# A hybrid attention, Fourier and long-convolution block: two opening blocks of one tile, the context's squares from its columns, and its norm factor ahead of the second filter's transform

## The chip, the core and the metric

The kernel runs on one core of a Trainium2 chip. A core has a matmul engine (TensorE, PE in the profile, with its weight loads as PEld), a vector engine (VectorE, DVE), an engine for activations and copies (ScalarE, ACT), a general engine (GpSimd, POOL) and a queue engine that issues most transfers (SyncE, SP). Each engine takes its instructions in a fixed order and waits where an operand is not there yet. Matmuls add up in PSUM, in eight banks of 128 x 512 fp32; everything else lies in SBUF, 128 partitions wide. The metric is the device time of one launch in microseconds; lower is better.

## The reference

One layer of a backbone over 256 latent tokens and 256 context tokens, 2048 channels wide, one sample, all in fp32. The change lies in the first step for both token sets, and in the filters of the long convolution:

```python
def rmsnorm(x, g):
    xf = x.astype(jnp.float32)
    y = xf * lax.rsqrt(jnp.mean(xf * xf, axis=-1, keepdims=True) + EPS)
    return (y * g.astype(jnp.float32)).astype(x.dtype)

def modulate(h, shift, scale):
    return h * (1 + scale) + shift

mod = (silu(c) @ ada_w + ada_b)            # 6 parts of 2048: sh1, sc1, g1, sh2, sc2, g2
mod_c = silu(c_ctx) @ ada_w + ada_b
h = modulate(rmsnorm(x, norm1_g), sh1, sc1)
hc = modulate(rmsnorm(ctx, norm1_g), csh1, csc1)
q, k, v, f, hy = split_projection(h @ w_in)
kc, vc = split(hc @ w_in[:, 1024:3072])
a = neighbourhood_attention(q, k, v, kc, vc, rpb)     # window keys and all context keys
y = merge_groups(a, fourier_mix(f), hyena_mix(hy, ...), mix_norm_g)
x = x + g1 * (y @ w_out)
x = x + g2 * conv_gated_mlp(modulate(rmsnorm(x, norm2_g), sh2, sc2), ...)
return rmsnorm(x, final_norm_g)
```

`hyena_mix` has two long convolutions. Each one's filter comes from a small sine network with a decay, and is used through its spectrum.

## The kernel before

Activations lie with channels on partitions: 16 tiles of 128 channels by 256 tokens. Every fp32 weight chunk is split in two by ScalarE (`w_hi`, a rounded copy, L173) and VectorE (`w_lo`, the rest, L174); an activation is split likewise (`hx_hi`, `hx_lo` of the latents, `hc_hi`, `hc_lo` of the context), and a product is three matmuls (`mm3`, L162).

The opening stage, which the change touches, makes keys and values for both token sets. It runs over blocks of channel tiles, `blocks=(2, 2, 4, 4, 4)`. For each block, the modulation (shift and scale of these channels) is first worked out from raw chunks of `ada_w`, in pieces (`prep_pieces`; products at L496 in four strips of 32 rows, `adasb` at L506, transposes at L170, the columns A1 and B1 at L515 and L516). Then `hprep` makes the activations of the block: `modulate` (L252, the tile `ht`), then `hi` on ScalarE (L256) and `lo` on VectorE (L257). Then four groups (`group`) multiply the block's tiles: two of keys, two of values. The first block's results are copied out of PSUM (L581), later ones added (L583). The pieces of the next block stand among the groups of the present one. A block of nk tiles takes 2 MB of modulation chunks for two tiles' width, and 1 MB of weights for each tile.

Ahead of the blocks stands a list of steps, `start` in `CFG`. `x0 x1` load the latents as pairs of tiles, `a00 a01 a10 a11` the first block's modulation chunks, `W` its first weights, `ct` the context a second time, by rows of tokens (2 MB into `kT`), `c0 c1` the context by channels. `q0` sums the latents' squares on PE through a matrix of ones; `q1` sums the context's by rows, with ScalarE's own accumulator (L461, `c_sq`). `n0` and `n1` make the norm factors; `n1` makes a factor for each token, and spreads it over partitions through a diagonal matrix `dg` (L226) and a matmul, to `rs_b` (L231). `f0` and `f1` make the two filters in time (`kz`, in the tile `v_t`, L436), and `s0` and `s1` their spectra (`fold`, four matmuls against `ftab`, a copy at L181 and four adds and subtractions at L184 to L188). `h0` and `h1` are `hprep` of the first block for the latents and the context, `e` a piece of its modulation, `w` its first weight split. A scheduler orders each engine's instructions from this list and their dependencies, so rows of one step stand between those of another.

Raw chunks of 512 KB go through eight buffers (`w_raw`) and three set aside for some modulation chunks (`a_raw`); a buffer is free when its chunk has been multiplied or split. Split weights have two buffers. SP issues loads in one order, and a load whose buffer is not free holds up all behind it. Sums in PSUM use five banks (`acc_ps`) and three (`mi_ps`).

After this stage come the other projections, the Fourier and long-convolution groups, attention, the output projection and the MLP, all on the same pattern. Another part of the modulation is made on VectorE (`ada_cols`, L351) beside the matmuls, and reads `s_row`, a row of activated conditions spread over partitions (`silu_row`, issued before the second block).

## Time and profile before

| | us |
|---|---|
| median of three runs | 1295.93 |
| lowest, highest | 1295.56, 1326.62 |
| the profiled execution | 1301.22 |
| its span | 1299.4 |

The profiled execution is one of its own, 5.3 us over the median of the runs. Its span runs from the first instruction to the last; 1.8 us lie around it.

| stage, us from the span's start | PE busy, us | granted clock | GB/s |
|---|---|---|---|
| 0 to 20 | 14.89 | 1.00 | 320 |
| 20 to 30 | 8.95 | 0.83 | 419 |
| 30 to 40 | 10.00 | 1.00 | 411 |
| 40 to 50 | 5.30 | 0.95 | 343 |
| 50 to 60 | 10.00 | 0.71 | 213 |
| 60 to 80 | 20.00 | 1.00 | 303 |
| 80 to 100 | 20.00 | 1.00 | 396 |

The columns come from windows of the profile. Busy time of PE counts the whole span of a matmul, with what its pipeline overlaps, so a full window does not mean that matmuls follow as closely as they can; the granted clock is the share of full speed at which PE may run. An fp32 matmul that is not split shows as two records. Rows of a timeline are: start, length, engine, line, operation, tile written and tiles read, count, and in brackets the idle time of the engine ahead of it with what ended it.

### The profile page before, as it was taken

What the parts mean: (1) busy time and instruction counts of PE and PEld (TensorE: products, weight loads), DVE (VectorE), ACT (ScalarE), POOL (GpSimd) and SP (SyncE); (2) the same over time, 40 slices, a digit from 0 to 9 for tenths busy, and PEclk for the clock granted to TensorE, in tenths of its full rate; (3) what the DMA queues carried; (4) which work ended last, traced back from release to release, by engine and by line L of the source; (5) the groups of instructions that cost most, each with busy time, mean ns of one, the idle gap of its engine ahead of it and who ended that gap; (6) DMA issues with size and microseconds to landing.
All of it is one profiled execution on the core that took longest, in us unless ns stands there. A gap on an engine that the chain in (4) does not pass through costs nothing.

```text
span 1299.4 us, 24490 instructions
## 1 busy us (share of the span) xinstructions
PE 1271.8 (98%) x10290; PEld 1197.3 (92%) x10290; DVE 886.5 (68%) x1301; ACT 558.5 (43%) x736; POOL 0.9 (0%) x7
## 2 busy tenths in 40 slices
PE   8899999999989999999999999999999999999997
PEld 5578788899989888999999999999999999999997
DVE  4447668958999897987676767744446555655663
ACT  4443212135333665455444444433334444454543
POOL 0000000000000000000000000000000000000000
PEclk9899999999999999999999999999999999999999
DMA  9887888988669875846877777855555656665541
GB/s 357 331 338 262 313 333 300 339 277 306 213 235 342 305 233 172 275 150 220 274 251 265 254 262 256 293 195 194 193 194 192 194 193 195 193 195 192 195 162 66
DMA packets 94015, 315.28 MB, mean 243 GB/s; under 512 B 16080, under 2 KB 16336, under 8 KB 93264
## 3 DMA queue, kind: packets, MB, share of 16 engines
q1 hardware_dynamic: 93328, 312.65, 69.5%
q8 instruction: 80, 1.31, 0.4%
q10 hardware_dynamic: 576, 1.07, 0.2%
q14 instruction: 31, 0.25, 0.1%
HBM read 311.58 MB, written 2.10 MB: 241 GB/s over the span
## 4 chain that ended last, share of the span: by engine, by line
PE 90%; DVE 5%; DMA 2%; ACT 1%; issue 1%; DVEq 0%; SPq 0%; ACTq 0%
PE acc_ps L162 83%; PE mi_ps L162 4%; PE mi_ps L496 2%; DVE w_lo L174 1%; DMA raw<-in_ada_col_t 1%; PE mi_ps L170 1%; DMA raw<-in_ada_t 1%; DVE raw L351 1%; DMA x_in<-in_xT 0%; ACT w_hi L173 0%; DMA hpack<-in_hpack 0%; DVE Y L768 0%; PE acc_ps L496 0%; DVE X L775 0%; DVE X L184 0%
## 5 line engine op out<-in xcount | busy, mean ns | idle before, releaser
L173 ACT CAST w_hi<-raw 128x1024 fp32r<-128x1024 f32 x376 | 381.1, 1051 | 524.2 <-PE acc_ps L162 457.6
L174 DVE TENSOR_TENSOR w_lo<-raw,w_hi 128x1024 fp32r<-128x1024 f32 x376 | 448.3, 1222 | 221.2 <-ACT w_hi L173 220.4
L162 PE MATMUL acc_ps<-h_hi,w_hi 128*128 128x256 f32 x1408 | 388.3, 276 | 0.5 <-ACT h_hi L256 0.5
L162 PE MATMUL acc_ps<-h_lo,w_hi 128*128 128x256 f32 x1408 | 388.6, 276 | 0.0
L162 PE MATMUL acc_ps<-h_hi,w_lo 128*128 128x256 f32 x1408 | 388.5, 276 | 0.0
L162 PEld LDWEIGHTS acc_ps<-h_hi,w_hi 128*128 128x128 f32 x1408 | 264.1, 188 | 0.7 <-ACT h_hi L256 0.7
L162 PEld LDWEIGHTS acc_ps<-h_lo,w_hi 128*128 128x128 f32 x1408 | 264.3, 188 | 0.0
L162 PEld LDWEIGHTS acc_ps<-h_hi,w_lo 128*128 128x128 f32 x1408 | 264.3, 188 | 0.0
L162 PE MATMUL acc_ps<-yh,w_lo 128*128 128x256 f32 x704 | 194.3, 276 | 0.0
L162 PE MATMUL acc_ps<-yh,w_hi 128*128 128x256 f32 x704 | 194.3, 276 | 0.0
L162 PE MATMUL acc_ps<-yl,w_hi 128*128 128x256 f32 x704 | 194.3, 276 | 0.0
L351 DVE SCALAR_TENSOR_TENSOR raw<-raw,s_row 128x1024 f32<-128x1024 f32 x128 | 154.8, 1223 | 39.1 <-DMA raw<-in_ada_col_t 39.0
L162 PE MATMUL acc_ps<-hx_hi,w_hi 128*128 128x256 f32 x512 | 145.6, 285 | 0.0
L162 PE MATMUL acc_ps<-hx_hi,w_lo 128*128 128x256 f32 x512 | 142.6, 281 | 1.0 <-DVE w_lo L174 1.0
L162 PE MATMUL acc_ps<-hx_lo,w_hi 128*128 128x256 f32 x512 | 143.2, 280 | 0.0
L162 PEld LDWEIGHTS acc_ps<-yh,w_hi 128*128 128x128 f32 x704 | 132.2, 188 | 0.0
L162 PEld LDWEIGHTS acc_ps<-yl,w_hi 128*128 128x128 f32 x704 | 132.2, 188 | 0.0
L162 PEld LDWEIGHTS acc_ps<-yh,w_lo 128*128 128x128 f32 x704 | 132.2, 188 | 0.0
L162 PEld LDWEIGHTS acc_ps<-hx_hi,w_hi 128*128 128x128 f32 x512 | 96.3, 188 | 8.1 <-issue 4.2
L162 PEld LDWEIGHTS acc_ps<-hx_lo,w_hi 128*128 128x128 f32 x512 | 96.5, 188 | 2.8 <-issue 2.4
L162 PEld LDWEIGHTS acc_ps<-hx_hi,w_lo 128*128 128x128 f32 x512 | 96.0, 189 | 2.1 <-DVE w_lo L174 1.4
L694 ACT ACTIVATE ga<-acc_ps,pack 128x256 f32<-128x256 f32 x44 | 23.8, 559 | 38.0 <-PE acc_ps L162 31.6
(237 smaller groups left out, 1532.0 us busy)
## 6 DMA issues: line engine op xcount, KB each, us to landing
raw<-in_ffn_t SPq DMA_DIRECT2D x264, 512.0 KB, 4.4
raw<-in_ada_col_t SPq DMA_DIRECT2D x128, 512.0 KB, 5.0
raw<-in_ada_t SPq DMA_DIRECT2D x64, 512.0 KB, 7.0
raw<-in_w_in_t SPq DMA_DIRECT2D x48, 512.0 KB, 5.5
raw<-in_w_kv_t SPq DMA_DIRECT2D x32, 512.0 KB, 5.9
raw<-in_w_out_t SPq DMA_DIRECT2D x32, 512.0 KB, 4.7
x_in<-in_xT SPq DMA_DIRECT2D x8, 256.0 KB, 5.4
kT<-in_c_tok SPq DMA_DIRECT2D x1, 2048.0 KB, 14.8
```

Of the source, the lines that this page charges most:

```text
L162: return nc.tensor.matmul(ps, lhsT, rhs, start=start, stop=stop, skip_group_check=True)
L170: nc.tensor.transpose(ps, src, ident[:n, :n])
L173: nc.scalar.copy(hi, src)
L174: TT(lo, src, hi.bitcast(F32), op=ALU.subtract)
L351: STT(r, r, 1.0, s_row[:, h * NA : (h + 1) * NA], op0=ALU.mult, op1=ALU.mult, accum_out=sums_[:, f, h : h + 1])
L496: return nc.tensor.matmul(ps[32 * j : 32 * j + 32, :w], s_t[:, kt, :], raws[i // nh][:, kt % nh, :], start=fresh, stop=q == last_q and i i ...
L694: nc.scalar.activation(dst, ps, AF.Identity, bias=b, scale=w1_)
```

## The change

The blocks become `(1, 1, 2, 4, 4, 4)`. A block of one tile takes one pair of modulation chunks for shift and one for scale, over 128 columns, and one weight chunk of 2048 columns, whose two halves are now columns and not tiles. The first two channel tiles of `x`, `ctx` and the low parts become tiles of their own, so that they can be used alone.

The load of the context by rows is gone. `q1` now squares the context's channel tiles on ScalarE and adds the squares on VectorE into one pair of tiles; `rms_bcast` then sums over channels with four matmuls against ones. In the list of steps `s1` moves from before `n1` to the end, behind `h1`; `ct`, `a01`, `a11` and two of the four `e` go.

```diff
-    p1=(0, 0, 2, 6, 9),
-    blocks=(2, 2, 4, 4, 4),
+    p1=(0, 0, 0, 2, 6, 9),
+    blocks=(1, 1, 2, 4, 4, 4),
...
-    start='hp pk x0 x1 h3 dc ft a00 a01 a10 a11 W wm si n1s wp n2s q0 ct c0 c1 e e n0 f0 e e h0 w s0 f1 s1 q1 n1 h1',
+    start='hp pk x0 x1 h3 dc ft a00 a10 W wm si n1s wp n2s q0 c0 c1 e n0 f0 e h0 w s0 f1 q1 n1 h1 s1',
...
         def add(self):
-            self.tiles.append(self.pool.tile([P, 2, L], self.dt, tag=self.pool.name, name=self.name, bufs=KT // 2))
+            if len(self.tiles) < 2:
+                t = self.pool.tile([P, 1, L], self.dt, tag=self.pool.name + "_1", name=self.name, bufs=2)
+            else:
+                t = self.pool.tile([P, 2, L], self.dt, tag=self.pool.name, name=self.name, bufs=KT // 2 - 1)
+            self.tiles.append(t)
...
-        def row_squares():
-            sums = p1.tile([P, 2], F32, name="c_sq")
-            for t in range(2):
-                nc.scalar.activation(c_tok[:, t], c_tok[:, t], AF.Square, accum_out=sums[:, t : t + 1])
-            return sums
+        def summed_squares():
+            for q in range(KT // 2):
+                sq = kT[:, q, :]
+                if q:
+                    nc.scalar.activation(sq.rearrange("p (k n) -> p k n", n=L), xs[1].tiles[q + 1][:], AF.Square)
+                    TT(kT[:, 0, :], kT[:, 0, :], sq, op=ALU.add)
+                else:
+                    for i in range(2):
+                        nc.scalar.activation(sq[:, i * L : (i + 1) * L], xs[1].tiles[i][:, 0], AF.Square)
+            return [kT[:, 0, i * L : (i + 1) * L] for i in range(2)]
...
-            rbs[v] = rms_bcast(p1, None, D, f"rs{v}", ps) if v else rms_rows(p1, ps[:, :L], D, f"rs{v}")
+            rbs[v] = rms_bcast(p1, ps, D, f"rs{v}") if v else rms_rows(p1, ps[:, :L], D, f"rs{v}")
...
-            own = ((0, 3), (0,))[m] if k0 == 0 else (0, 3, 5)
+            own = ((0,), (0,))[m] if k0 == 0 else (0, 3, 5)
...
-                if k % 2:
+                if k < 2 or k % 2:
                     lo.add()
...
-            "ct": lambda: nc.sync.dma_start(c_tok, a["c_tok"].rearrange("(t p) n -> p t n", p=P)),
```

`own` names the modulation chunks that go to the three buffers set aside. The list `p1` gets a zero for the added block: the same side work (`ada_cols`) stands beside the three large blocks.

What the change moves shows best in the order of instructions. First SP, from the start of the program; `x_in` are the tiles of the latents and the context, `spec`, `v_t` and `ftab` take the filters' tables. Before:

```order
L383 DMA x_in<-in_xT 128x512 x8
L598 DMA spec<-in_hy_w 64x2x512 x2
L605 DMA v_t<-in_hy_decay 128x2x512
L606 DMA ftab<-in_dft_f 128x512
L268 DMA raw<-in_ada_t 128x1024 x8
L268 DMA raw<-in_w_kv_t 128x1024 x2
L610 DMA kT<-in_c_tok 128x2x2048
L383 DMA x_in<-in_cT 128x512 x8
```

After:

```order
L613 DMA spec<-in_hy_w 64x2x512 x2
L620 DMA v_t<-in_hy_decay 128x2x512
L621 DMA ftab<-in_dft_f 128x512
L267 DMA raw<-in_ada_t 128x1024 x4
L267 DMA raw<-in_w_kv_t 128x1024 x2
L392 DMA x_in<-in_cT 128x256 x2
L392 DMA x_in<-in_cT 128x512 x7
L267 DMA raw<-in_w_kv_t 128x1024 x2
L267 DMA raw<-in_ada_t 128x1024 x4
L415 DMA s_row<-in_c_row 128x2048
```

The context's tiles stand behind six chunks now, not behind ten and the 2 MB of rows; the second block's weights and modulation, and the row `s_row`, follow directly.

Second VectorE, around the context's norm factor (`rs_m` to `rs_b`); `spec` rows are the second filter's transform. Before:

```order
L221 TENSOR_SCALAR rs_m<-c_sq 128x2
L184 TENSOR_TENSOR spec<-mi_ps,v_t 128x512
L186 TENSOR_TENSOR spec<-mi_ps,v_t 128x512
L184 TENSOR_TENSOR spec<-mi_ps,v_t 128x512
L188 TENSOR_TENSOR spec<-v_t,mi_ps 128x512
L194 RECIPROCAL rs_r<-rs_s 128x2
L195 SCALAR_TENSOR_TENSOR rs_s<-rs_r,rs_m 128x2
L196 TENSOR_TENSOR rs_s<-rs_s,rs_r 128x2
L197 SCALAR_TENSOR_TENSOR rs_r<-rs_s,rs_r 128x2
L226 TENSOR_SCALAR dg<-pack,rs_r 128x128 x2
L231 COPY rs_b<-mi_ps 128x256
L174 TENSOR_TENSOR w_lo<-raw,w_hi 128x1024
```

After, from the third add of squares (`kT`) on:

```order
L474 TENSOR_TENSOR kT<-kT 128x512
L174 TENSOR_TENSOR w_lo<-raw,w_hi 128x1024 x2
L445 TENSOR_TENSOR v_t<-mi_ps,v_t 128x512 x2
L474 TENSOR_TENSOR kT<-kT 128x512 x4
L220 TENSOR_SCALAR rs_m<-mi_ps 128x2
L194 RECIPROCAL rs_r<-rs_s 128x2
L195 SCALAR_TENSOR_TENSOR rs_s<-rs_r,rs_m 128x2
L196 TENSOR_TENSOR rs_s<-rs_s,rs_r 128x2
L197 SCALAR_TENSOR_TENSOR rs_r<-rs_s,rs_r 128x2
L225 TENSOR_SCALAR dg<-pack,rs_r 128x128 x2
L230 COPY rs_b<-mi_ps 128x256
L251 SCALAR_TENSOR_TENSOR ht<-x_in,A_68,rs_b 128x256
```

The four transform rows and the split have left the way from the squares to `ht`; seven adds, two splits of the second block's weights and the second filter's products have come ahead of it.

Third PE, from the last products on the latents' activations to the first on the context's. Before:

```order
L162 MATMUL acc_ps<-hx_hi,w_lo 128x256
L162 MATMUL mi_ps<-dg,ones 128x128 x2
L162 MATMUL acc_ps<-hc_hi,w_hi 128x256 x5
L162 MATMUL acc_ps<-hc_lo,w_hi 128x256
L162 MATMUL acc_ps<-hc_hi,w_lo 128x256
L496 MATMUL mi_ps<-raw,s_t 32x256 x8
```

After:

```order
L162 MATMUL acc_ps<-hx_hi,w_lo 128x256
L162 MATMUL mi_ps<-ones,kT 128x1 x4
L162 MATMUL mi_ps<-dg,ones 128x128 x2
L162 MATMUL mi_ps<-v_t,ftab 128x512 x3
L162 MATMUL acc_ps<-hc_hi,w_hi 128x256 x5
L162 MATMUL mi_ps<-v_t,ftab 128x512
L512 MATMUL mi_ps<-raw,s_t 32x128 x16
```

The column sums stand ahead of the broadcast, three of the second transform's four products between it and the first context product, and the next block's modulation is 16 narrow products in one piece. On ScalarE, around the root (L193) of the same factor, the row `s_row` is activated ahead of `hc_hi`:

```order
L473 ACTIVATE kT<-x_in 128x512 x2
L173 CAST w_hi<-raw 128x1024 x2
L193 ACTIVATE rs_s<-rs_m 128x2
L416 ACT_TABLE_LOAD
L416 ACTIVATE s_row<-s_row 128x2048
L255 ACTIVATE hc_hi<-ht,B_69 128x256
L181 COPY v_t<-mi_ps 128x512 x2
```

Before, the casts stand behind the root, and `s_row` is activated later, behind the second block's activations:

```order
L461 ACTIVATE kT,c_sq<-kT 128x2048 x2
L181 COPY v_t<-mi_ps 128x512 x2
L193 ACTIVATE rs_s<-rs_m 128x2
L173 CAST w_hi<-raw 128x1024 x2
L256 ACTIVATE hc_hi<-ht,B_69 128x256 x2
```

So the root of the factor now waits for the second block's weights, and `hc_hi` for the row.

More of the change, by code (lines that the diff above doesn't have):

```diff
@@ L212, in busy, with rms_bcast @@
                 mm(ps[:, :P], ones[:], ones[:], True, True)
-    def rms_bcast(pool_, sqs, n, name, ps=None, fill=None):
-        if ps is None:
-            ps = bank()
-            last = col_sums(ps, sqs)
-            if fill:
-                busy(last, fill[0])
+    def rms_bcast(pool_, sqs, n, name, fill=None):
+        ps = bank()
+        last = col_sums(ps, sqs)
+        if fill:
+            busy(last, fill[0])
         ms = pool_.tile([P, 2], F32, name=f"{name}_m", tag=f"{name}_m")
@@ L273, in loads @@
             for q in range(2):
-                z = (slice(None), slice(q * nk // 2, (q + 1) * nk // 2))
-                raws.append((z, self.load(src[2 * i + q], nk // 2, n)))
+                if nk == 1:
+                    z = (slice(None), slice(None), slice(q * n // 2, (q + 1) * n // 2))
+                    raws.append((z, self.load(src[2 * i + q], 1, n // 2)))
+                else:
+                    z = (slice(None), slice(q * nk // 2, (q + 1) * nk // 2))
+                    raws.append((z, self.load(src[2 * i + q], nk // 2, n)))
             return raws
@@ L378, in hybrid_block @@
     hs = ((hx_hi, hx_lo), (hc_hi, hc_lo))
-    xs = [Pairs(z, F32, "x_in", KT // 2) for z in (x_pool, c_pool)]
+    xs = [Pairs(z, F32, "x_in", KT // 2 + 1) for z in (x_pool, c_pool)]
     def load_pairs(dst, src, q):
-        for j in range(4 * q, 4 * q + 4):
-            nc.sync.dma_start(dst.tiles[j][:], src[:, 2 * j * L : (2 * j + 2) * L].rearrange("p (k n) -> p k n", n=L))
+        for j in range(5 * q, 5 + 4 * q):
+            k0, k1 = (j, j + 1) if j < 2 else (2 * j - 2, 2 * j)
+            nc.sync.dma_start(dst.tiles[j][:], src[:, k0 * L : k1 * L].rearrange("p (k n) -> p k n", n=L))
     def load_x(dst, src, q):
@@ L450, in squares @@
                 sq = kT[:, q, :].rearrange("p (k n) -> p k n", n=L)
-                nc.scalar.activation(sq, xs[0].tiles[q][:], AF.Square)
+                if q:
+                    nc.scalar.activation(sq, xs[0].tiles[q + 1][:], AF.Square)
+                else:
+                    for i in range(2):
+                        nc.scalar.activation(sq[:, i], xs[0].tiles[i][:, 0], AF.Square)
                 for i in range(2):
@@ L496, in product @@
                         return nc.tensor.matmul(ps[32 * j : 32 * j + 32, :w], s_t[:, kt, :], raws[i // nh][:, kt % nh, :], start=fresh, stop=q == last_q and i in ends, skip_group_check=True)
-                    ends = range(4) if n2 == 8 else range(n2)
+                    ends = {16: range(4, 8), 8: range(4)}.get(n2, range(n2))
                     last_raw = product(nh)
@@ L535, in hprep @@
                 ts.append((modulate(p1, xs[vv][:, k, :], A, rbs[vv][:]), B, hi[:, k, :]))
-                if k % 2:
+                if k < 2 or k % 2:
                     lo.add()
-                    for i in range(2):
-                        t, B, h = ts[i]
-                        shift_split(t, B, h, lo[:, k - 1 + i, :])
+                    for i, (t, B, h) in enumerate(ts):
+                        shift_split(t, B, h, lo[:, k - len(ts) + 1 + i, :])
                     ts = []
@@ L592, in sq @@
         def sq(v):
-            parts[v] = row_squares() if v else squares()
+            parts[v] = summed_squares() if v else squares()
         def load_w3():
@@ L627, in hybrid_block @@
             for g in range(4):
-                while todo and n0 - len(todo) < n0 * (g + 1) / (3 if blocks[b][1] == 2 else 4):
+                while todo and n0 - len(todo) < n0 * (g + 1) / (3 if blocks[b][1] <= 2 else 4):
                     todo.pop(0)()
@@ L1016, in tiled @@
         for i, (w, k, nk, c, n) in enumerate(chunks):
-            nk //= halves
+            by_cols = halves == 2 and nk == 1
+            if by_cols:
+                n //= 2
+            else:
+                nk //= halves
             for q in range(halves):
-                z = inp[w][0, (k + q * nk) * P : (k + (q + 1) * nk) * P, c : c + n]
+                if by_cols:
+                    z = inp[w][0, k * P : (k + 1) * P, c + q * n : c + (q + 1) * n]
+                else:
+                    z = inp[w][0, (k + q * nk) * P : (k + (q + 1) * nk) * P, c : c + n]
                 out[halves * i + q] = z.reshape(nk, P, n).transpose(1, 0, 2).reshape(P, nk * n)
@@ L1029, in laid_out @@
     r["ada_col_t"] = np.concatenate([w[:, p * D : (p + 1) * D].T.reshape(KT, P, 2, NA).transpose(0, 2, 1, 3).reshape(2 * KT, P, NA) for p in SIDE_PARTS])
-    r["c_tok"] = inp["ctx"][0]
     r["c_row"] = inp["c"].reshape(1, D)
```

7 lines of the change are left out of this document (5 added, 2 removed).

## Prediction

> **What bounds the kernel now.** I read the page first (busy shares, and the chain that ended last by engine), then the waits of the matmul engine in the first 300 us, where the whole change lies, then the windows around the last of these waits, and the chain in order of time.
>
> ```profile
> span 1299.4 us, 24490 instructions
> PE 1271.8 (98%) x10290; PEld 1197.3 (92%) x10290; DVE 886.5 (68%) x1301; ACT 558.5 (43%) x736; POOL 0.9 (0%) x7
> PE 90%; DVE 5%; DMA 2%; ACT 1%; issue 1%; DVEq 0%; SPq 0%; ACTq 0%
> ...
> PE acc_ps L496 <- DMA raw<-in_ada_t: 2.7, 2, 1.3
> PE acc_ps L162 <- ACT hc_hi L256: 2.6, 1, 2.6
> PE mi_ps L162 <- DVE dg L226: 2.1, 1, 2.1
> PE mi_ps L170 <- ACT adasb L506: 1.0, 2, 0.5
> ```
>
> The kernel is a stream of matmuls, 90% of its chain. Only the opening is not: in 300 us, PE's three largest waits are for the first modulation chunks, and twice for the context's norm factor (dg, then the first context activations hc_hi). No wait behind those three is over 1.0 us, and none comes later than hc_hi. So the change can win only ahead of that point, and must not lose behind it.
>
> ```profile
> 43.50:49.20 5.70, 1.00 (x8) 0.64 (x6) 4.88 (x13) 0.89 (x3) 0.00 (x0) 0.98 0.85 344
> 49.20:55.80 6.60, 6.60 (x35) 4.86 (x36) 1.73 (x3) 1.44 (x3) 0.00 (x0) 0.50 0.19 52
> 55.80:65.20 9.40, 9.40 (x100) 7.24 (x100) 1.45 (x7) 4.39 (x9) 0.00 (x0) 1.00 1.02 422
> ...
> 11.01 8.96 DMA raw<-in_ada_t
> ...
> 43.51 0.69 DVE spec L184
> ...
> 45.50 0.30 DVE dg L226
> ...
> 45.93 0.70 PE mi_ps L162 x4
> ...
> 49.20 2.19 PE acc_ps L162 x7
> ```
>
> PE works 1.0 of the 5.7 us ahead of 49.20, and then runs at a granted clock of 0.50 until 55.80: the idle time is paid a second time, by half of 6.6 us, that is 3.3 us. From 49.20 on it does not stop. The reason for the late factor is VectorE's order, not its work:
>
> ```profile
> 44.12 0.68 DVE L188 TENSOR_TENSOR spec<-v_t,mi_ps 128x512 f32<-128x512 f32 x1
> 44.72 0.16 DVE L194 RECIPROCAL rs_r<-rs_s 128x2 f32<-128x2 f32 x1
> ...
> 46.99 1.22 DVE L174 TENSOR_TENSOR w_lo<-raw,w_hi 128x1024 fp32r<-128x1024 f32 x1
> 48.12 0.88 DVE L252 SCALAR_TENSOR_TENSOR ht<-x_in,A,rs_b 128x256 f32<-128x256 f32 x2
> ...
> 33.71 1.91 ACT L461 ACTIVATE kT<-kT 128x2048 f32<-128x2048 f32 x1 [0.47 <-DMA kT<-in_c_tok]
> 41.73 0.21 ACT L193 ACTIVATE rs_s<-rs_m 128x2 f32<-128x2 f32 x1
> ```
>
> The squares of the context rows start at 33.71, when the rows land; the reciprocal waits behind the second filter's transform (the L188 add ends at 44.80), and one weight split stands between the broadcast and the modulation.
>
> **The change, step by step.**
>
> *Loads.* Two MB of context rows go, and the first block needs 4 modulation chunks, not 8, so the context tiles come 4 MB earlier in SP's order. In the profile the fourth chunk lands at 11.01 + 8.96 = 19.97, after the same loads as in the changed order.
>
> ```profile
> 20.00:30.00 10.00, 8.95 (x61) 4.20 (x62) 4.58 (x12) 1.25 (x3) 0.00 (x0) 0.83 1.03 419
> ...
> 18.84 0.38 SPq L610 DMA_DIRECT2D kT<-in_c_tok  x1
> 19.99 14.04 SPq L383 DMA_DIRECT2D x_in<-in_cT  x8
> ```
>
> At 419 GB/s a 512 KB chunk takes 1.25 us. Behind 19.97 come two weight chunks and the context (as much as four): landed at 27.5; the next block's two weight chunks at 30.0. Splitting a 256 KB tile in two adds one issue for x and one for the context; SP issues far ahead there, so I cost them at nothing; without that cover it would be two issues of 0.3 us.
>
> *Sums of squares.* Two activations over 2048 columns go. In come nine on ScalarE and seven adds on VectorE, and four column sums on PE.
>
> ```profile
> L451 ACT ACTIVATE kT<-x_in 128x512 f32<-128x512 f32 x8 | 4.5, 619 | 2.0 <-DMA x_in<-in_xT 2.0
> L461 ACT ACTIVATE kT<-kT 128x2048 f32<-128x2048 f32 x2 | 3.8, 1906 | 0.5 <-DMA kT<-in_c_tok 0.5
> L173 ACT CAST w_hi<-raw 128x1024 fp32r<-128x1024 f32 x4 | 4.1, 1043 | 0.0
> ...
> L710 DVE TENSOR_TENSOR sqf<-sqf 128x512 f32<-128x512 f32 x2 | 1.4, 693 | 2.0 <-ACT sqf L709 2.0
> ...
> 296.40 0.95 PE L162 MATMUL mi_ps<-ones,sqf 128*128 128x1 f32 x8
> ```
>
> ScalarE pays 4.5 for 3.8, beside the arriving tiles (8 x 0.56; its last square ends about 31), then casts the next block's weights (2 x 1.0, to about 33). VectorE's order decides: behind those casts stand two splits (1.22 each, to about 35), two products of the second filter and then the last four adds. Such 0.69 us operations start 0.61 apart (43.51 and 44.12), so 6 x 0.61 = 3.7 brings the sum to 38.7. Column sums (0.95 and two hand-offs) and the root (0.21) lead to the reciprocal at about 40.8; from reciprocal to broadcast the profile takes 45.93 - 44.72 = 1.2, so the broadcast starts at 42.0, 3.9 earlier than now.
>
> *Factor in front of the transform.* The split between broadcast and modulation is gone, but PE's order now has three transform products there, and ScalarE's a table load and the silu row between the root and hc_hi.
>
> ```profile
> 29.99 2.58 PE mi_ps L162 x6
> ...
> 71.16 1.28 ACT L407 ACT_TABLE_LOAD   x1
> 72.46 1.92 ACT L407 ACTIVATE s_row<-s_row 128x2048 f32<-128x2048 f32 x1
> ```
>
> The products take 2.58, so the first context matmul starts at about 42.5 + 2.6 = 45.1; the silu row (its load lands at 30.0 + 4 chunks + 2.5 = 37.5) is done about 43.6, and hc_hi at 44.1, just in time. Against 49.20 that is 4.1 us won.
>
> *What PE has not yet done at that point.* Before, 30 latent matmuls and the whole transform lay ahead of it; now 15 and three quarters.
>
> ```profile
> 41.21 0.92 PE acc_ps L162 x8
> ...
> 56.70 1.00 PE mi_ps L496 x16
> ...
> 58.36 0.27 PE mi_ps L170 x2
> ...
> 66.72 9.87 PE acc_ps L162 x43
> ...
> 76.58 1.85 PE mi_ps L496 x16
> ```
>
> Fifteen matmuls at 0.92/8 = 0.115 are 1.7; one transform product is 2.58/3 = 0.86. Six blocks instead of five give one more set of modulation products: 32 products, 64 records, for one tile, each over 128 columns, which the trace does not have. At 512 columns a record costs 1.85/16 = 116 ns, at 256 it costs 62; the line through both gives 35 ns at 128, 2.2 us; half of 62 gives 2.0, no gain from narrowing at all 4.0. I take 2.2, by the line, and keep 2.0 and 4.0. Nothing excludes that the two narrow blocks of 128 overlap better than the line, but both bounds come from the same four-strip products. The Trainium skill, page "TensorE: Matmul & The Clock Gate", Part 1, states that matmuls never start less than about 25 ns apart however narrow they are; by that 64 records are at least 1.6 us as an estimate, 0.6 less than my term, and it would not bind at 35 ns. Transposes of one more block 0.3. Together 1.7 + 0.9 + 2.2 + 0.3 = 5.1 us given back.
>
> *The clock.* Before, the halved clock costs 3.3. In the new order PE is again without work from the end of the 15 matmuls (about 34.6) to the column sums (38.8), 4.2 us. A like case is in the trace, where PE waits in the long convolution:
>
> ```profile
> 383.50:386.90 3.40, 1.02 (x8) 1.04 (x8) 3.40 (x6) 0.00 (x0) 0.00 (x0) 1.00 0.00 0
> 386.90:390.30 3.40, 3.40 (x17) 3.32 (x17) 2.92 (x5) 0.00 (x0) 0.00 (x0) 0.50 0.17 34
> ```
>
> One stretch of 3.4 us at 0.50 follows, worth 1.7; the wait at 43.5 brought two, worth 3.3. I take 1.7, as the new gap is nearer to the shorter; the bounds are 0 and 3.3. The same page and part of the Trainium skill states that a window of about 3.4 us without matmuls halves the clock and that one busy window restores it. By that rule it is one stretch here, 1.7, and the sum is as below; the 6.6 us at 0.50 behind 49.20 speak against it, and by that row the sum would be 1.6 higher, 1296.9.
>
> *Sum.* Won 4.1 + 3.3 = 7.4; paid 5.1 + 1.7 = 6.8: 0.6 us faster. The profiled execution took 1301.22 us, 5.3 above the median of the three runs, 1295.93; against the median this is 1295.3.
>
> *Behind the opening.* Blocks of one tile have half the work to cover the same steps: 48 x 0.115 + 24 x 9.87/43 = 11.0 us each. I cost this at nothing, covered by prefetch: SP runs ahead by up to 11 chunks. If that cover is gone, the rivals below.
>
> **The rivals.**
>
> *Slower: the second block cannot feed the third.* Two tiles' modulation weights (4 MB) and two MB of weights must come in while PE works 11.0 us plus four modulation pieces of 1.00, 15 us, and one raw buffer of the three set aside is freed only when the third block's first piece has been multiplied, with SP's whole queue behind it. Six MB at 419 GB/s are 15 us, so it decides where the prefetch is under about four chunks.
>
> ```profile
> 80.00:100.00 20.00, 20.00 (x151) 14.26 (x147) 9.23 (x18) 0.59 (x1) 0.00 (x0) 1.00 1.00 396
> ```
>
> For it: at 80 to 100, where blocks of two become blocks of four, the transfers already run at 396 GB/s. Against it: even there PE does not wait. Price: two to four chunks, 2.5 to 5 us, so 1298 to 1301.
>
> *VectorE becomes the bound in the second block.* Sixteen adds at 0.61 (9.8), two splits (2.4), eight modulation steps at 0.44 (half of 0.88; 3.5) are 15.7 against PE's 15. Against it: five banks let the adds lag. Price 1 to 2 us, so 1296.5 to 1297.5.
>
> *More is won.* The clock is not halved (the column sums and the broadcast break the gap), which gives 1.7 more, and the last adds come up to 2 us sooner, when the weights land sooner. For it: VectorE has work for 4.58 of 10 us at 20 to 30. Against: its order holds the adds behind the weight splits whatever ScalarE does. Price 2 to 4 us more: 1291 to 1293.
>
> **How the numbers follow.** My forecast, 1295.3 with 2.5 us either way, has 0.45; more won 0.23; starved third block 0.22; VectorE bound 0.10. The range takes the rivals in and what a median moves: 1289.5 to 1301.5. A measurement of this kernel can tell about 2%, 26 us, from no change; none of the cases reaches that, since PE's idle time and halved clock before 49.20 hold less that could be won: faster 0.01, same 0.97, slower 0.02.
>
> **What would show it.** The first matmul on hc_hi at 44 to 47 us, not 49.2; the reciprocal of the context's factor near 41, with seven adds ahead of it; one or two stretches at 0.50 near 42 to 49; modulation records of 128 columns near 35 ns; no PE wait for raw chunks between 50 and 110. Wrong would be: hc_hi before 42 (VectorE's order does not bind) or after 48, or waits of PE for the modulation chunks in the third or fourth block.

## The result and the profile after

| | us |
|---|---|
| median of the changed kernel, five runs | 1304.7 |
| median of the kernel before, run beside it, five runs | 1296.78 |
| ratio, 95% interval | 1.0053 [1.0031, 1.0074] |
| the profiled execution, its span | 1304.7, 1302.9 |

By the ratio the change costs 0.53% of 1296.78 us: 6.9 us, by the interval 4.0 to 9.6. The time, 1304.7 us, lies outside the forecast's range (1289.5 to 1301.5); that it would not differ from before by 2% was right. Any kernel here has executions that run some 2% longer from 560 us on; the ratios leave them out, and where a profile caught one (s1_back, cols_factor, after_aligned, columns_alone, aligned_again), only its first 300 us are used.

First the head of the page of the changed kernel, the busy time of the engines and the chain that ended last by engine, then PE's longest waits in the first 300 us (total, count, longest):

```profile
span 1302.9 us, 24690 instructions
PE 1274.6 (98%) x10362; PEld 1201.6 (92%) x10362; DVE 902.8 (69%) x1332; ACT 558.8 (43%) x744; POOL 0.9 (0%) x7
PE 92%; DVE 4%; DMA 2%; ACT 1%; issue 0%; SPq 0%; DVEq 0%; ACTq 0%
...
PE mi_ps L162 <- DVE kT L474: 4.5, 1, 4.5
PE mi_ps L170 <- ACT adasb L522: 3.0, 2, 2.6
PE acc_ps L512 <- DMA raw<-in_ada_t: 1.8, 1, 1.8
PE mi_ps L162 <- DVE dg L225: 1.6, 1, 1.6
```

The wait for hc_hi (2.6 us before) is gone. In its place PE waits 4.5 us for kT, the sum of the context's squares, more than for anything else. (The wait for adasb, where ScalarE's copy stands behind the first squares, is 0.4 us in after_again, and the additions end no earlier there; it does not count.) VectorE and PE around that wait, in order of time, and then PE in windows of 3.4 us (after the length comes PE's busy time; the granted clock is the figure ahead of the last two):

```profile
33.39 2.35 DVE L174 TENSOR_TENSOR w_lo<-raw,w_hi 128x1024 fp32r<-128x1024 f32 x2
35.66 1.28 DVE L445 TENSOR_TENSOR v_t<-mi_ps,v_t 128x512 f32<-128x512 f32 x2
36.86 2.86 DVE L474 TENSOR_TENSOR kT<-kT 128x512 f32<-128x512 f32 x4
41.68 0.16 DVE L220 TENSOR_SCALAR rs_m<-mi_ps 128x2 f32<-128x2 f32 x1 [1.96 <-PE mi_ps L162]
42.11 0.17 DVE L194 RECIPROCAL rs_r<-rs_s 128x2 f32<-128x2 f32 x1 [0.27 <-ACT rs_s L193]
...
39.77 1.87 PE L162 MATMUL mi_ps<-ones,kT 128*128 128x1 f32 x8 [4.50 <-DVE kT L474]
43.24 1.22 PE L162 MATMUL mi_ps<-dg,ones 128*128 128x128 f32 x4 [1.59 <-DVE dg L225]
44.25 5.08 PE L162 MATMUL mi_ps<-v_t,ftab 128*128 128x512 f32 x6
48.59 1.34 PE L162 MATMUL acc_ps<-hc_hi,w_hi 128*128 128x256 f32 x5
```

```profile
35.30:38.70 3.40, 0.00 (x0) 0.00 (x0) 3.33 (x6) 0.00 (x0) 0.00 (x0) 1.00 0.99 402
38.70:42.10 3.40, 1.87 (x8) 1.78 (x8) 1.15 (x3) 0.21 (x2) 0.00 (x0) 0.50 1.03 411
42.10:45.55 3.45, 2.31 (x6) 1.69 (x7) 2.04 (x8) 3.26 (x3) 0.00 (x0) 0.50 0.84 335
45.55:48.95 3.40, 3.40 (x6) 1.35 (x4) 1.46 (x3) 1.02 (x2) 0.00 (x0) 0.50 0.03 11
48.95:52.40 3.45, 3.45 (x46) 2.27 (x44) 1.60 (x3) 0.98 (x3) 0.00 (x0) 1.00 0.00 0
```

The queue is the one forecast: two splits, two products of the second filter, then the last four additions, which end at 39.7. PE does nothing for a whole window, and the clock stays at a half for three, 38.7 to 48.95 (for two in after_again and after_third, 39.6 to 46.4 and 40.1 to 46.9). The column sums and the three transform products, which were to hide the modulation, run at half speed in them; the products take 48.59 - 44.25 = 4.3 us instead of 2.58 (3.1 and 3.3 us with two halved windows). So the first context matmul is at 48.59, not at 45.1.

### The profile page after: what moved, and what is told of

It reads as the page before. It is cut to its first block, busy times and chain, and to the rows that moved or that the text cites. A ratio compares the mean times of both kernels' runs of the same rounds, so it can differ in the third digit from the quotient of the medians.

```text
span 1302.9 us, 24690 instructions
## 1 busy us (share of the span) xinstructions
PE 1274.6 (98%) x10362; PEld 1201.6 (92%) x10362; DVE 902.8 (69%) x1332; ACT 558.8 (43%) x744; POOL 0.9 (0%) x7
## 4 chain that ended last, share of the span: by engine, by line
PE 92%; DVE 4%; DMA 2%; ACT 1%; issue 0%; SPq 0%; DVEq 0%; ACTq 0%
PE acc_ps L162 84%; PE mi_ps L162 5%; PE mi_ps L512 2%; PE mi_ps L170 1%; DMA x_in<-in_cT 1%; DMA raw<-in_w_out_t 1%; DMA raw<-in_ada_t 1%; DVE w_lo L174 1%; ACT w_hi L173 0%; DMA x_in<-in_xT 0%; DVE Y L782 0%; DVE raw L359 0%; DVE kT L474 0%; DVE X L184 0%; DVE X L784 0%
## 5 line engine op out<-in xcount | busy, mean ns | idle before, releaser
L708 ACT ACTIVATE ga<-acc_ps,pack 128x256 f32<-128x256 f32 x44 | 23.7, 558 | 37.7 <-PE acc_ps L162 31.6
```

What stands on the lines that cost most here:

```text
L708: nc.scalar.activation(dst, ps, AF.Identity, bias=b, scale=w1_)
```

## Experiments

The table has the kernels run. "At 64" says whether the context's activations lie on multiples of 64 bytes. The three times are read from each kernel's profiled execution: the start of the first context matmul, of the last matmul of the first two channel tiles ("two tiles"; the expectations call it the 192nd), and of the first Fourier product. The ratio is to the kernel before on the same chip; different rows can be of different chips.

| kernel | blocks | squares | factor | at 64 | ratio, 95% | context | two tiles | Fourier |
|---|---|---|---|---|---|---|---|---|
| before | 2, 2 | rows | behind | yes | | 49.2 | 76.2 | 280.8 |
| before_again | 2, 2 | rows | behind | yes | | 47.5 | 73.2 | 278.2 |
| changed | 1, 1 | columns | in front | no | 1.0053 [1.0031, 1.0074] | 48.6 | 78.2 | 284.8 |
| after_again | 1, 1 | columns | in front | no | 1.0056 [1.0032, 1.0080] | 47.7 | 77.1 | 283.7 |
| after_third | 1, 1 | columns | in front | no | 1.0038 [1.0002, 1.0075] | 48.0 | 77.3 | 283.9 |
| s1_back | 1, 1 | columns | behind | no | 1.0039 [1.0019, 1.0060] | 47.6 | 74.9 | 281.5 |
| cols_factor | 2, 2 | columns | in front | no | 1.0068 [1.0034, 1.0103] | 57.1 | 78.9 | 285.5 |
| blocks_alone | 1, 1 | rows | behind | yes | 0.9980 [0.9964, 0.9996] | 39.0 | 68.2 | 274.1 |
| rows_factor | 1, 1 | rows | in front | yes | 0.9972 [0.9956, 0.9988] | 37.4 | 67.3 | 273.2 |
| factor_alone | 2, 2 | rows | in front | yes | 0.9953 [0.9935, 0.9971] | 44.3 | 68.4 | 274.9 |
| columns_alone | 2, 2 | columns | behind | yes | 1.0006 [0.9993, 1.0019] | 57.1 | 78.7 | 282.3 |
| after_aligned | 1, 1 | columns | in front | yes | 1.0017 [1.0005, 1.0029] | 48.9 | 77.9 | 283.5 |
| aligned_again | 1, 1 | columns | in front | yes | 1.0030 [0.9991, 1.0068] | 48.2 | 77.5 | 282.2 |
| aligned_filled | 1, 1 | columns | in front | yes | 0.9973 [0.9947, 1.0000] | 47.4 | 75.8 | 280.6 |
| adds_first | 1, 1 | columns | in front | yes | 1.0049 [1.0016, 1.0082] | 46.7 | 78.4 | 284.0 |
| before_shifted | 2, 2 | rows | behind | no | 1.0012 [0.9998, 1.0025] | 47.7 | 74.7 | 281.0 |
| rows_factor_shifted | 1, 1 | rows | in front | no | 1.0004 [0.9980, 1.0028] | 38.8 | 68.8 | 276.3 |

### Both kernels again

No edit.

> The kernel before, unchanged, to see which of its parts vary. The profiled execution of before took 1301.2 us, its other undisturbed runs 1295.6 to 1296.8. Theory A (the loss lies in the opening): the new profile is again about 1301 and the opening is the same, first context matmul at 49.2 and 0.50 of the clock from there for 6.8 us. Theory B (the profiled execution of before was an unlucky one of several): the new profile is at 1296 to 1298 and is shorter somewhere by 3 to 5 us, either in the opening (one halved stretch less) or in the pace of the matmuls.

> The changed kernel, unchanged. Both theories: 1304 to 1305 us. Theory A: first context matmul at 48 to 49 and three halved stretches ahead of it, as in the first profile. Theory B: the number of halved stretches varies between executions (one to three), and the time with it by 1.7 us for each.

The ratio stands: 1.0056. But the kernel before is not the one of the first profile. Its window 20 to 30 us, at a granted clock of 0.83 in that profile, is here:

```profile
20.00:30.00 10.00, 8.96 (x65) 4.09 (x59) 7.29 (x20) 3.10 (x6) 0.00 (x0) 1.00 1.02 419
```

The first execution lost 1.7 us there to a stretch of half clock (0.17 of 10 us), which this one did not have. Its context matmuls start at 47.50 instead of 49.20, and two tiles are done at 73.2 instead of 76.2. That is theory B, and it holds for the changed kernel too, whose gap is followed by two halved windows in after_again and by three in the first profile: the number goes with the execution.

### The factor back behind, and blocks of two with columns

In s1_back the changed kernel has `s1` where it was; cols_factor has blocks of two tiles, with the columns and the moved factor.

```diff
-    start='... w s0 f1 q1 n1 h1 s1',
+    start='... w s0 f1 s1 q1 n1 h1',
```

```diff
...
-    blocks=(1, 1, 2, 4, 4, 4),
+    blocks=(2, 2, 4, 4, 4),
...
-    start='... c0 c1 e n0 f0 e h0 w s0 f1 q1 n1 h1 s1',
+    start='... c0 c1 e e n0 f0 e e h0 w s0 f1 q1 n1 h1 s1',
...
```

> The changed kernel with the second filter's transform again in front of the context's factor in the list of steps. Theory A (the transform behind the factor runs at the halved clock and costs 2 to 3 us there): the four products run at full clock in PE's gap before the column sums, the gap is shorter than 3.4 us, the first context matmul comes at 45 to 47, and the time falls by 2 to 4 us to 1301 to 1303. Rival (VectorE is what binds): the transform's four VectorE operations, 2.5 us, stand ahead of the last adds, the factor comes 2.5 us later, and the time is the same or up to 2 us longer.

> Blocks as before (2, 2, 4, 4, 4), with the squares from the columns and the factor in front of the transform. Theory A (the small blocks give back about 5 us of matmul work and modulation behind the first context matmul, and win little): 1296 to 1300 us, so 4 to 8 below the changed kernel. Rival (columns and factor are what costs, through VectorE's adds and the halved clock): 1303 to 1306, like the changed kernel.

Both are slower than before: neither the moved factor nor the narrow blocks is what the loss hangs on. For cols_factor that is the rival, against theory A. Common to them and to the changed kernel are the columns and, as it turned out, the address of the context's activations. With the columns, the factor in front does not win. s1_back is done with two tiles 2.1 us sooner than after_again, and the median of the runs that the ratio uses is 1.7 us lower (1302.2 against 1303.9): a time within its theory A, though the context starts at 47.6, not by 47. The ratios, 1.0039 and 1.0056, have intervals that overlap.

### Rows in place of columns

Three kernels have the squares from rows, with c_sq and the load `ct` as before: blocks_alone (one-tile blocks), rows_factor (and the factor in front), factor_alone (blocks of two, only the factor moved). The fourth, columns_alone, is before with the columns, and with an empty tile that holds the addresses. Their lists of steps, from the context's load on:

```diff
 blocks_alone
+    start='... ct c0 c1 e n0 f0 e h0 w s0 f1 s1 q1 n1 h1',
 rows_factor
+    start='... ct c0 c1 e n0 f0 e h0 w s0 f1 q1 n1 h1 s1',
 factor_alone
-    start='... ct c0 c1 e e n0 f0 e e h0 w s0 f1 s1 q1 n1 h1',
+    start='... ct c0 c1 e e n0 f0 e e h0 w s0 f1 q1 n1 h1 s1',
 columns_alone
+    start='... c0 c1 e e n0 f0 e e h0 w s0 f1 s1 q1 n1 h1',
```

> The first two blocks of one tile each, but the context's squares from its rows, loaded again, and the factor of the second filter ahead of the square's sum, as before; c_sq is there, so the addresses are before's. Theory F (what the narrow blocks cost behind the opening): from 60 matmuls of the key and value product to 192, 17.8 us in before and 20.4 in both kernels with one-tile blocks that were run, so 2.6 us longer here too, of which 0.7 us come back in the third block; the opening as in before, since the load of the rows still ends last; ratio 1.001 to 1.002. Rival G (the one-tile blocks let the first matmuls start sooner, as the change meant): ratio 0.998 to 1.000.

> One-tile blocks and the factor in front of the second filter's transform as in the change, but the context's squares from its rows, loaded again; addresses as before. With the one-tile blocks alone the rows landed at 28.5 us, their squares ended at 32.6, the first context matmul began at 39.0 and the first two tiles' matmuls ended at 68.2, with no halved clock in the opening; the changed kernel's nine additions ended at 39.7 and its two tiles at 77.1 and 78.2. Theory H (the columns cost the opening: their additions stand in VectorE's queue behind the splits of the weights and the filters, TensorE runs dry and its clock is halved): here too the first context matmul comes by 40 us and the two tiles end at 67 to 70, ratio 0.996 to 0.999. Rival I (the factor's place costs it: the transform's products run between broadcast and first context matmul): first context matmul not before 43, two tiles after 72, ratio 1.000 or more.

> The kernel before with only the context's factor put in front of the second filter's transform (squares from rows, blocks of two tiles). In before the row sums' mean is on VectorE at 37.2 us and the reciprocal waits behind four steps of the transform until 42.9. By the prediction's own step the reciprocal comes at some 40 us, the broadcast at 41 and, behind three or four transform products of 0.43 us each at the full clock or 0.85 at half, the first context matmul at 43 to 46 instead of 47.5 to 49.2: two tiles' end 71 to 73, ratio 0.998 to 0.9995. Rival L (the products that now stand between broadcast and context take what the earlier factor won): first context matmul 47 or later, ratio 1.000 to 1.002.

> Blocks of two tiles and the order of before, with the context's squares from its columns added on VectorE and no load of the rows; an empty tile of 32 bytes holds the addresses. Theory H: the additions end no earlier than the rows' squares did (reciprocal 42.9 us in before), with twice the modulation to wait for; first context matmul 48 to 56 us (57.1 with the factor moved too), two tiles' end 75 to 79 (before 73.2 and 76.2), ratio 1.001 to 1.005. Rival J (the columns land 0.6 us a tile earlier than the rows and win that): first context matmul 44 to 47, ratio 0.998 to 0.9995.

These three with rows are all faster than before; all kernels with the columns are slower or the same, except the one whose gap was filled (below). rows_factor does what theory H said, and factor_alone wins more than expected. Against theory F and for G, blocks_alone starts the context at 39.0. The fewer modulation chunks bring the rows themselves earlier. ScalarE, VectorE and PE in blocks_alone, and VectorE and PE in factor_alone:

```profile
30.60 1.90 ACT L475 ACTIVATE kT<-kT 128x2048 f32<-128x2048 f32 x1
33.20 0.16 DVE L221 TENSOR_SCALAR rs_m<-c_sq 128x2 f32<-128x2 f32 x1
36.02 0.69 PE L162 MATMUL mi_ps<-dg,ones 128*128 128x128 f32 x4
39.02 0.85 PE L162 MATMUL acc_ps<-hc_hi,w_hi 128*128 128x256 f32 x5 [0.72 <-ACT hc_hi L256]
```

```profile
39.58 0.17 DVE L194 RECIPROCAL rs_r<-rs_s 128x2 f32<-128x2 f32 x1 [0.27 <-ACT rs_s L193]
40.71 0.71 PE L162 MATMUL mi_ps<-dg,ones 128*128 128x128 f32 x4 [0.27 <-DVE dg L226]
41.26 3.60 PE L162 MATMUL mi_ps<-v_t,ftab 128*128 128x512 f32 x8
44.30 0.68 PE L162 MATMUL acc_ps<-hc_hi,w_hi 128*128 128x256 f32 x1
```

By rows ScalarE makes the squares and their sums in one pass, which ends at 32.5 in blocks_alone; the last addition of the changed kernel ends at 39.7. In factor_alone the reciprocal no longer waits for the transform (39.58 against 44.72), and PE runs the four transform products in 44.30 - 41.26 = 3.0 us, at full clock. What that does to PE shows in windows from 30 to 50 us of the changed kernel, of rows_factor and of factor_alone (figures as above):

```profile
30.00:40.00 10.00, 5.50 (x25) 3.43 (x24) 9.47 (x14) 3.07 (x5) 0.00 (x0) 0.94 1.02 412
40.00:50.00 10.00, 8.41 (x24) 5.38 (x25) 3.97 (x12) 5.08 (x6) 0.00 (x0) 0.55 0.51 205
```

```profile
30.00:40.00 10.00, 9.56 (x50) 6.54 (x49) 7.82 (x19) 6.29 (x12) 0.00 (x0) 1.00 1.04 421
40.00:50.00 10.00, 9.95 (x106) 7.82 (x106) 4.26 (x14) 8.18 (x18) 0.00 (x0) 1.00 1.01 413
```

```profile
30.00:40.00 10.00, 10.00 (x45) 6.21 (x45) 8.96 (x19) 7.46 (x11) 0.00 (x0) 1.00 1.03 408
40.00:50.00 10.00, 9.73 (x68) 6.91 (x68) 7.63 (x15) 5.82 (x10) 0.00 (x0) 1.00 0.81 331
```

PE is busy for 13.9 of 20 us in the changed kernel and for 19.5 and 19.7 in the others, and in those two its clock is full there. At the end of two tiles rows_factor is 10.1 and 10.6 us ahead of the two traces of the aligned kernel (after_aligned and aligned_again), which differs from it in the squares and the load that they need. Over the whole kernel less of it is left: 0.9972 against 1.0017 and 1.0030, 5.8 to 7.5 us.

The narrow blocks add nothing to the moved factor (0.9972 against 0.9953, with intervals that overlap). columns_alone is between its two theories: its context is as late as H said (57.1), but the ratio is that of no change. So the columns by themselves, in the old order and blocks, cost nothing that these runs can tell; what they cost beside the other two parts is the distance above. Its opening is that of cols_factor (57.1, and two tiles at 78.7 against 78.9), so beside the columns the factor's place moves nothing in the opening of blocks of two. Their ratios lie further apart (1.0006, and 1.0068 from two runs) than the address accounts for; why stays open. Some of what an opening wins or loses goes where PE next meets the loads. PE's waits from 262 to 340 us, in rows_factor and then in before_again:

```profile
PE acc_ps L162 <- DVE w_lo L174: 1.4, 1, 1.4
PE mi_ps L162 <- DVE sqf L723: 0.2, 1, 0.2
```

```profile
PE mi_ps L162 <- DVE dg L226: 0.2, 1, 0.2
```

The early kernels wait 1.4 us for a split weight that the kernel before found ready. From the Fourier stage to the last matmul rows_factor then takes 3.2 us more than before_again; but the first execution of before takes 2.7 more than its second there, so most of this can lie between executions of one kernel. Part of it is the clock once more: rows_factor runs at 0.50 from 555.1 for 3.4 us, seven of the twelve profiles that are used beyond 300 us have such a stretch from some point between 554 and 566 us on, and of the two executions of before only the first does. The rest I have not followed.

### Is it the idle stretch, and VectorE's order?

Both kernels are the changed one with addresses put back. aligned_filled puts 20 products of ones by ones into PE's gap; adds_first moves the sum of squares ahead.

```diff
+        def fill_gap(n):
+            ps = bank()
+            for _ in range(n):
+                mm(ps[:, :P], ones[:], ones[:], True, True)
...
-    start='... e h0 w s0 f1 q1 n1 h1 s1',
+    start='... e h0 w s0 f1 fl q1 n1 h1 s1',
```

```diff
-    start='... e h0 w s0 f1 q1 n1 h1 s1',
+    start='... e h0 q1 n1 w s0 f1 h1 s1',
```

> The kernel with the addresses put back, and 20 products of ones by ones (128 x 128, some 0.21 us each by the four of the broadcast that took 0.84 us) in TensorE's gap between the transform's first products at 33 us and the column sums of the squares at 39.8 us, where it was idle for 4.5 us. They write a bank that nothing reads. Theory C (the opening was lost to the halved clock, not to a wait): with no idle stretch there the granted clock stays at 1.0, the column sums take 1.0 us instead of 1.87, the three transform products 1.5 us rather than 3.1 to 4.3, and the end of the first two tiles' matmuls (78.15 and 77.06 us in the changed kernel's two profiles) comes 1.7 to 3.3 us earlier than in the aligned kernel without them. Rival D (the opening waits on VectorE and ScalarE for hc_hi): first context matmul not before 47 us, and less than 0.7 us won. Rival E: the products delay the first matmuls of x and the column sums, and it is slower.

> The changed kernel with the addresses put back and the context's sum of squares moved ahead of the first weight pair's second splits, the first filter's transform and the second filter: on VectorE the nine additions then follow each other behind x's low parts, and the two splits, the four transform additions and the filters come after them; on TensorE the first filter's last eight products stand between the broadcast and the first context matmul. Theory H: the additions end near 33 us instead of 39.7 (the last square ends at 31.1), the broadcast is at 36 to 38, TensorE has no idle stretch over 2 us and keeps its clock, the two tiles end at 70 to 73 instead of 77 to 78, ratio 0.997 to 0.9995. Rival K (what is moved behind costs as much: TensorE's queue waits for the transform's additions between broadcast and context): two tiles' end 75 or later, ratio 1.001 or more.

PE in aligned_filled, and its windows:

```profile
33.57 4.63 PE L162 MATMUL mi_ps<-ones 128*128 128x128 f32 x40
...
39.64 1.05 PE L162 MATMUL mi_ps<-ones,kT 128*128 128x1 f32 x8
42.29 1.22 PE L162 MATMUL mi_ps<-dg,ones 128*128 128x128 f32 x4 [1.60 <-DVE dg L225]
...
38.60:42.00 3.40, 2.06 (x17) 1.77 (x15) 1.81 (x8) 0.20 (x1) 0.00 (x0) 0.99 0.99 405
42.00:45.40 3.40, 3.11 (x7) 2.03 (x8) 1.34 (x4) 0.15 (x1) 0.00 (x0) 0.50 0.09 36
45.40:48.80 3.40, 3.40 (x35) 1.84 (x37) 1.68 (x3) 3.37 (x4) 0.00 (x0) 1.00 0.02 5
```

Work that computes nothing makes the kernel faster: 0.9973 against 1.0017 for after_aligned on the same chip. The column sums take 1.05 us instead of 1.87, the broadcast comes 1.0 earlier than in the changed kernel, one window behind the gap is at half clock instead of two or three, and two tiles are done 1.7 and 2.1 us before the aligned kernel's two traces. That is theory C at its lower end, since one window stays halved. By the ratios the gain is 5.7 us, by the medians of the runs that they use 4.3 (1296.7 against 1301.0); what it is made of beyond the opening's 1.7 to 2.1 no trace shows. D's condition held (the first context matmul is at 47.4), its price didn't. The filling is not all that differs: the scheduler also put the fourth transform product and some of the modulation ahead of most of the context's matmuls, and `s_row` behind hc_hi on ScalarE. hc_hi was ready at 46.25, so neither order of ScalarE held PE up.

adds_first was expected by theory H to win, and did not. PE and VectorE there:

```profile
32.06 1.87 PE L162 MATMUL mi_ps<-ones,kT 128*128 128x1 f32 x8 [0.49 <-DVE kT L474]
37.33 1.22 PE L162 MATMUL mi_ps<-dg,ones 128*128 128x128 f32 x4 [3.40 <-DVE dg L225]
38.34 5.51 PE L162 MATMUL mi_ps<-v_t,ftab 128*128 128x512 f32 x8
...
34.05 1.23 DVE L174 TENSOR_TENSOR w_lo<-raw,w_hi 128x1024 fp32r<-128x1024 f32 x1
35.19 0.16 DVE L194 RECIPROCAL rs_r<-rs_s 128x2 f32<-128x2 f32 x1
...
35.66 1.23 DVE L174 TENSOR_TENSOR w_lo<-raw,w_hi 128x1024 fp32r<-128x1024 f32 x1
...
28.50:42.20 13.70, 9.67 (x30) 6.82 (x29) 8.12 (x19) 4.25 (x7) 0.00 (x0) 0.50 1.02 420
```

The additions end at 32.0, 7.7 us sooner, and the broadcast is 5.9 sooner. But with the transform moved behind, PE has still less to do meanwhile: its clock is a half for 13.7 us, the transform is paid at half speed, and two tiles are done at 78.4. (The ratio of 1.0049 is 1.0033 by the medians.) The edit does not clear VectorE's order altogether: the two splits now stand between the mean and dg, which lies 3.0 us behind the mean here and 1.2 in the changed kernel. What it shows is that earlier additions alone do not win, against my theory H. In both orders the column path leaves PE without work, and PE runs its next work at half speed; an order with neither additions nor splits in the way was not run.

### Thirty-two bytes

Without the tile c_sq everything in its pool, and in the pools below it, lies 32 bytes higher: hc_hi at 118304 instead of 118272. An empty tile of 32 bytes puts that back, or, in kernels that have c_sq, does the same harm. Each engine's order of instructions is the same with the tile and without it, in the traces of after and after_aligned as in those of before and before_shifted; that it moves instructions behind the Fourier stage, as the expectation of aligned_again has it, is not so.

```diff
-PADS = {"edge": 224, "p1": 0, "att": 224, "ffn": 160}
+PADS = {"edge": 224, "p1": 32, "att": 224, "ffn": 160}
```

> The changed kernel with one empty tile of 32 bytes in the pool that held the removed c_sq. Without c_sq everything in that pool and the ones below it lies 32 bytes higher; this puts hc_hi, hc_lo and s_t back on multiples of 64 bytes, where they are in the kernel before. The order of instructions is the changed kernel's. Theory A (the 32 bytes): in the changed kernel's two traces the context's matmuls of 256 columns start 117 to 118 ns apart and those of 512 columns 233.4 ns; with the addresses back they should be 113 to 116 and 229, in 384 and 192 matmuls of the four-tile blocks that is 384 x 2.5 ns + 192 x 4.4 ns = 1.8 us, and up to 2.6 us where they are at 113 throughout: ratio to before some 1.0035 to 1.0042 where the changed kernel had 1.0056. Rival B (the pace comes from the blocks' order or from chance): the spacing stays at 117 to 118 and 233, ratio 1.005 to 1.006. The first product of the Fourier stage, 192 matmuls at 113 ns in both traces of before and at 117.7 ns in all four of changed kernels, has the same operand addresses in all: by A it stays at 117.7.

> The kernel before with the same empty tile of 32 bytes, which here moves hc_hi, hc_lo and s_t 32 bytes off the multiples of 64, as the change does, and changes nothing else. Theory A: the context's matmuls go to 117 to 118 and 233 ns apart, 1.8 to 2.6 us more, ratio 1.0014 to 1.002; the opening, up to the end of the first two blocks of work, as before (first context matmul 47.5 to 49.2 us). Rival B: no difference, ratio 1.000, spacing 113 to 116 and 229.

> The changed kernel once more, beside the next kernel on the same chip. Theory A (the 32 bytes cost 1.0 to 1.8 us, which is what the traces show from the 192nd matmul to the Fourier stage: 206.6 us in four kernels that lie 32 bytes off, 204.6 to 205.6 in four that don't): ratio 1.003 to 1.006, and 0.0008 to 0.0014 over the next kernel's. Rival M (they cost some 5 us, the distance of the two ratios measured so far on different chips, 1.0056 and 1.0017): the two kernels differ by 0.003 or more.

> The changed kernel with the empty tile of 32 bytes, once more. Theory A: 0.0008 to 0.0014 below the changed kernel's ratio; by its trace 205 to 205.7 us from the 192nd matmul to the Fourier stage and first context matmul at 47.5 to 49. Rival M: 0.003 or more below it, with time won behind the Fourier stage, where the tile also moves some of ScalarE's and VectorE's instructions in the order.

> One-tile blocks, squares from rows and the factor in front, with the empty tile of 32 bytes, which here moves hc_hi, hc_lo and s_t off the multiples of 64. Without it the ratio was 0.9972 and the way from the 192nd matmul to the Fourier stage 205.8 us. Theory A: 206.8 to 207.6 us there, ratio 0.998 to 0.9986. Rival M: ratio 1.000 or more. Rival B (no cost of the addresses): 205.8 and 0.997.

The last of the context's matmuls of 512 columns, in a row, in before_again (21 rows from the first to the last shown), after_again (19) and after_aligned (21):

```profile
251.43 0.39 PE L162 MATMUL acc_ps<-w_hi,hc_hi 128*128 128x512 f32 x1
...
256.00 0.39 PE L162 MATMUL acc_ps<-w_hi,hc_lo 128*128 128x512 f32 x1
```

```profile
256.50 0.40 PE L162 MATMUL acc_ps<-w_hi,hc_lo 128*128 128x512 f32 x1
...
260.70 0.39 PE L162 MATMUL acc_ps<-w_hi,hc_lo 128*128 128x512 f32 x1
```

```profile
255.98 0.39 PE L162 MATMUL acc_ps<-w_hi,hc_hi 128*128 128x512 f32 x1
...
260.56 0.39 PE L162 MATMUL acc_ps<-w_hi,hc_lo 128*128 128x512 f32 x1
```

The starts lie 4.57 / 20 = 0.2285 us apart, then 4.20 / 18 = 0.2333, and with the tile 4.58 / 20 = 0.2290 again. Those of 256 columns, from 100 us on, lie 113 to 116 ns apart on average in the ten traces of kernels at 64, and 117 to 118 in the seven of kernels that are not. It adds up: from the end of the first two tiles to the last of these matmuls the changed kernel takes 183.6 us in each of its three traces; 182.6, 181.8 and 181.8 with the addresses put back (after_aligned, aligned_again, aligned_filled); before_shifted takes 184.1, before 182.4 and 182.8; rows_factor_shifted 185.3, rows_factor 183.7. So 32 bytes cost 1.0 to 1.9 us, in each of three pairs of kernels, and rival B is out. The ratios are too wide to size it. before_shifted has 1.0012, and side by side on one chip 1.0038 and 1.0030 speak against rival M, but rest on two runs of each that count; rows_factor_shifted is at 1.0004, where M put it, 0.0032 over rows_factor on another chip and with intervals that overlap. Its trace is where theory A put it: 207.5 us from two tiles to the Fourier stage.

The Fourier stage's first product behind it took 22.2 us in before and 23.0 in the changed kernel. As theory A said, it stays at 23.0 with the addresses put back. It is 23.0 in factor_alone too, and 22.2 in rows_factor and in both shifted kernels. What sets these 0.8 us stays open.

## Why the prediction was wrong, step by step

- *Loads, and VectorE's queue*: nearly right. The last squares, casts and splits end within a us of the forecast (31, 33, 35), the additions at 39.7 instead of 38.7 (40.0 and 40.1 in the two other executions).
- *Column sums to broadcast*: forecast 42.0, measured 43.24. The additions' delay is 1.0 of it and the half speed of the column sums 0.9 (1.87 us instead of 0.95); the hand-offs took 0.7 less than allowed.
- *Factor in front*: the products were where forecast, between broadcast and context, but at half speed: 48.59 instead of 45.1, past the 48 that the prediction named as a sign of being wrong (47.7 and 48.0 in the other two). hc_hi was ready at 46.0 and did not hold them up, nor did the casts hold up the root, which waited for VectorE's mean. That the factor's place itself wins is right, and more than forecast: factor_alone is 0.47% faster, 6.1 us.
- *What is given back*: right. From the first context matmul to the end of two tiles, halved clock taken off at half its length, before took 27.0 - 3.3 = 23.7 and 25.7 - 1.9 = 23.8, the changed kernel 29.6 - 0.2 = 29.4: 5.6 more against the forecast's 5.1. The narrow modulation records cost 1.08 us for 32 in the row below, whose successor starts 1.01 later; that is 32 ns, for 35 in the forecast.

```profile
50.72 1.08 PE L512 MATMUL mi_ps<-raw,s_t 128*32 128x128 f32 x32
51.73 0.39 PE L162 MATMUL acc_ps<-hc_lo,w_hi 128*128 128x256 f32 x1
```

- *The base*: the step that failed, and the largest part of the miss. "Won 4.1 + 3.3 = 7.4" took 49.20, and two stretches of half clock, as what the kernel before loses. Its other execution starts the context at 47.5 and ends two tiles at 73.2. Of the 7.4 that was to be won, 3.0 is what that one execution lost against the other; taking the sum off the median did not mend that.
- *The clock*: a term of the sum that was too small. "One stretch of 3.4 us at 0.50 follows, worth 1.7" was taken from a wait after which PE had work without a break. Here the wait is followed by column sums, a hand-off of 1.6 us and a broadcast, in which PE is busy for 1.87 and 2.31 us of a window, and two or three windows stay halved. Column sums, broadcast and transform took 3.3 us more than at the full clock in the profile, some 2 in the two other executions. The forecast end of two tiles, 76.2 - 4.1 - 3.3 + 5.1 + 1.7 = 75.6, came at 77.1 to 78.2: 1.5 to 2.6 us late, 1.0 to 1.4 of it through the additions and 0.2 to 1.6 through the clock (the hand-offs and what is given back nearly cancel). The rule weighed there, of the Trainium skill, page "TensorE: Matmul & The Clock Gate", Part 1, that one busy window restores the clock, agrees with the trace: the first window that PE fills (45.55 to 48.95) is the last halved one. What failed is the reading that the gap is followed by one.
- *Behind the opening, "I cost this at nothing"*: the third that failed. No starved third block, as the waits show, which puts that rival away; the bound on VectorE in the second block did not appear either. But a removed tile moved the context's activations, 1.0 to 1.9 us, and the first Fourier product took 0.8 more.

Together 3.0, 1.5 to 2.6, 1.0 to 1.9 and 0.8 are 6.3 to 8.3; by the ratio the forecast missed by 6.9 + 0.6 = 7.5 us (the time itself lies 9.4 over the 1295.3). That the columns, beside the other two parts, are what to leave out was not in it at all: the forecast asked how early they make the factor, and saw PE idle meanwhile, but not how early the rows would come with fewer chunks ahead of them.

## What to carry to other kernels

A change of several parts is costed part by part, and run part by part: here two parts each win alone (0.9980 and 0.9953), the third alone changes nothing that can be told (1.0006), and all three together lose (1.0053), so what each is worth depends on the others. One profile of the kernel before is not a base for a sum of a few us: two of its executions lay 3.0 us apart in the opening. An early result is worth only what the bound engine can do until it comes; where a step takes that engine's work away ahead of a wait, the wait is paid twice, by its idle time and by the slow clock of what follows. Removing a small tile moves what lies beside it, so addresses are compared before and after, like instructions.

## What was not expected of the hardware

The clock was halved not only by an idle window. In aligned_filled PE was busy for 2.06 of the 3.40 us from 38.60 to 42.00, and the next window was at 0.50. So windows that are partly filled can cost too, and a gap is better closed than shortened. They do not always: in the changed kernel PE was busy for 1.57 of the 3.41 us from 14.83 to 18.24, and the next window was at 1.00. What decides stays open. The Trainium skill, page "TensorE: Matmul & The Clock Gate", Part 1, puts the halving to an idle window of about 3.4 us; by this window, less than that is enough.

Activations 32 bytes past a multiple of 64 make the matmuls that read them start a few nanoseconds later each (233 ns apart instead of 229 with 512 columns), 1.0 to 1.9 us in all: that the address matters is shown by three pairs of kernels, why it does is not.
